# A two-layer conv/pool trunk on one core: low parts by subtraction, a later spill of x, and another place for the statistics of B's layer norm

## The chip, the cores and the metric

One NeuronCore of a Trainium2 chip runs the whole program. The metric is the device time of one execution in microseconds; the kernel before took 1789.1, 1791.0 and 1783.0 us in three runs (median 1789.1). Engines are named as the profile names them: PE is TensorE, DVE is VectorE, ACT is ScalarE, POOL is GpSimd, SP is SyncE, which issues most of the loads.

## What is computed

`x` is 1024 tokens by 1024 channels, fp32. Layer 0 mixes tokens with a Conformer convolution, layer 1 with a multi-scale pool; each is followed by a dense SwiGLU feed-forward of inner size 2816. Every sub-layer is normalized, shifted and scaled by numbers that come from a conditioning vector `c`.

```python
def conformer_conv(h, w1, b1, w_dw, b_dw, ln_g, ln_b, w2, b2):
    u = h @ w1 + b1
    a, g = jnp.split(u, 2, axis=-1)
    u = a * jax.nn.sigmoid(g)
    u = lax.conv_general_dilated(u, w_dw[:, None, :], ..., feature_group_count=D_MODEL) + b_dw   # 31 taps
    u = jax.nn.silu(layer_norm(u, ln_g, ln_b))
    return u @ w2 + b2

def swiglu_ffn(h, w_gate, w_up, w_down):
    return (jax.nn.silu(h @ w_gate) * (h @ w_up)) @ w_down

def reference(x, c, ada_w, ada_b, ...):
    c_act = jax.nn.silu(c)
    for i in range(DEPTH):
        mod = c_act @ ada_w[i] + ada_b[i]
        sh_m, sc_m, g_m, sh_f, sc_f, g_f = jnp.split(mod, N_ADA, axis=-1)
        h = modulate(rms_norm(x, norm_mix_g[i]), sh_m, sc_m)
        y = conformer_conv(h, ...) if i % 2 == 0 else multiscale_pool(h, ...)
        x = x + (1.0 + g_m)[:, None, :] * y
        h = modulate(rms_norm(x, norm_ffn_g[i]), sh_f, sc_f)
        x = x + (1.0 + g_f)[:, None, :] * swiglu_ffn(h, ...)
    return rms_norm(x, final_g)
```

## The kernel before, in words

**Tiles and products.** Channels lie on partitions, tokens along the free axis, in two chunks A and B of 512 tokens. A value that goes into TensorE is split into a high part, rounded to the matmul type by ScalarE, and a low part, the rest. Every product (`products`, L458) is then three matmuls of 128x128 by 128x512: high by high, high by low, low by high. These three are a row in what follows.

**Weights.** `load_weight` (L443) brings a slice of 128x1024 in fp32 into one of three `raw` buffers, and ScalarE casts it into the high part of one of five weight slots. The low part comes in one of two ways. With `summed=True`, ScalarE writes the negated copy of raw as the low part's input and a second DMA, issued by GpSimd's queue, loads the same slice again and accumulates it (tile `w<-in_..._dram`). Otherwise a subtract does it (`w<-raw,w`), on VectorE or GpSimd, whichever is free first by the program's model (`either`, L161). `run_units` (L591) decides: a unit names its weights, and a plain source is loaded with `summed=True`, while a callable in its place is called. Down weights are callables, and all others but the joint ones are plain sources.

**Order.** The program is written as a list of units that stands in TensorE's order: heads, down products, mixers. Work beside them (taps of the convolution, norms, the dots of `c` with the conditioning weights) is a generator that gives up control with a word. `pace` (L198) steps these while VectorE's or GpSimd's modelled clock is less than 4 us ahead of TensorE's. A word of `LOAD` holds a task back for that many us of the modelled clock, a word of `DELAY` (`DELAY_BEHIND` late in the program) until that long after its last instruction. `STRETCH` multiplies the modelled price of the taps of chunk B in the feed-forward of layer 0. The other engines' order comes from a list scheduler.

**Stages around the change.** Layer 0: `heads` computes pairs of gate and up slices (tile `p`, weights `wgu`) for A and B in rounds of four pairs, and after each round the down products of A (`dn<-g,w`, weights `wdn`). In the meantime the taps of B run on VectorE (`ca`) and on GpSimd and ScalarE (`pa`, `pr`). Then `layer_norm_silu` (L786) normalizes B over channels: a matmul with ones gives the mean, VectorE subtracts it (`u<-u,mean`), squares are added (`acc`), a matmul gives the variance, twelve small VectorE operations its inverse root, and another matmul spreads it (`rstd<-ident,col`); VectorE scales, ScalarE applies silu, and the high and low parts (`v`) go into the products with w2 (`conv_out`, L841, tile `y<-v,w`). After that come `whole` and `combinations` (L1098), which make sums of A's and B's halves, and the joint feed-forward of both chunks (`joint`, L1033, tiles `a`, `e`), down products of A and B, the pool of A beside the down products of B (`pool_h`, `pool_mixed`, L885, and `pool_out`, L911: tiles `win`, `mx`, `y<-mx,w`, weights `wpl`), the heads of layer 1 with the pool of B beside them, and again combinations, joint and down products. `ending` (L1214) is the last down product, with its own order.

**Spill.** `x_out` (L304) stores a chunk's x in four DMAs (`xd<-x`) on SP's queue, and `x_in` brings it back later; the buffers serve the combinations in between.

**Dots.** For layer 1, VectorE multiplies 48 slices of the conditioning weights with `c` (`adaw<-adaw,cact`); each slice is loaded by SP. They run from the joint stage of layer 0 on.

Of the kernel before, what the change touches and what calls it, by code (L numbers as in the profile page):

```python
# [38 lines left out]
ROUND = 4  # L39
# [12 lines left out]
DIAGS = 8  # L52
LOAD = {"load": 4.0, "slow": 6.0, "next": 4.0, "dots": 4.0}

ON_DVE = (1, 4)
AHEAD = 4
STRETCH = 1.35
LATER = 300
DELAY = {"stats": 2.75, "spread": 3.0}
DELAY_BEHIND = {"stats": 8, "spread": 4}  # L60

# [59 lines left out]
def trunk(ctx, tc, xT, c, vec, ada, adan, w1f, w1, wdg, w2, wgu, wdn, wpl, out):  # L121
# [356 lines left out]

    def mean_rsqrt(acc, n, keep=False):

        count = n // P
        yield "stats"
        b = bank("var")
        for i in range(count):
            matmul(b[:, i : i + 1], acc[:, i * P : (i + 1) * P], ones[:, 0:1], start=True, stop=True)
        v, t = b[:, :count], b[:, 16 : 16 + count]
        V_.tensor_scalar(v, v, EPS, None, op0=ADD)  # L490
        col = tmp.tile([P, 16], F32, tag="col1", name=nm("col"), bufs=1)[:, :count]
        yield from rsqrt(v, col, t)
# [95 lines left out]
    def unit(emit, *weights):  # L588
        units.append((weights, emit))

    def run_units(cap, early):  # L591
# [194 lines left out]
    def layer_norm_silu(ch):  # L786

        n = ch.n
        vs = [st["u", ch.i, k][:, HALO:] for k in range(KT)]
        acc = None  # L790
# [10 lines left out]
        if ch.i:  # L801
            calm[0], stretch[0] = True, 1.0
            clock["V"] = clock["G"] = clock["PE"]
        yield "stats"
        b = bank("mean")
# [7 lines left out]
        acc = yield from sum_sq([vs[k] for k in CENTRED], n)  # L813
        rstd = yield from mean_rsqrt(acc, n)
        S_.activation(tmp.tile([P, 16], F32, tag="col0", name=nm("col"), bufs=1)[:, 0:1], acc[:, 0:1], AF.Silu)
# [25 lines left out]
    def conv_out(ch, squares, then=None):  # L841
# [17 lines left out]
        for ds in [(0, 1), *((d,) for d in range(2, KT))]:  # L859
            unit(emit_of(ds), *[w2[d] for d in ds])  # L860
            if then is not None and len(ds) > 1:
                unit(then)
# [48 lines left out]
    def pool_out(ch, l, pair, sq):  # L911
        def emit(take):
            wt = take()
            for gi in range(2):
# [8 lines left out]
                pace()  # L923
        unit(emit, wpl[pair])

# [19 lines left out]
    def gated(l, i, f, g, u, kept=False):  # L945

        t = temp(512)
        S_.activation(t, g, AF.Silu)
        V_.tensor_tensor(t, u, t, op=MUL)
        both = block("u0", "g")  # L950
        split(t, both)
        if kept:
            st["g", i, f] = both[:, 0], both[:, 1]
        else:
            sync.dma_start(gd[l][i][f], both.bitcast(F32))

    def head(l, fp, kept=False):
# [24 lines left out]

        return (first, wgu[l, fp, 0]), (second, wgu[l, fp, 1])

# [113 lines left out]
    def combinations(l, squares):  # L1098

        hb = st["hb"] = [block("h1", "hb", F32) for _ in range(4)]  # L1100
        T = st["T"] = {name: {} for name in ("t1", "t2", "n3", "b22", "n4")}
        rstd = yield from mean_rsqrt(squares.acc, 512)
        lk = l * KT
# [84 lines left out]
    def down(ch, l, fs, then=()):  # L1188
# [19 lines left out]
        wd = []  # L1208
        unit(half(0, wd), *[lambda f=f: load_weight(wdn[l, f]) for f in fs])
        for emit in then:  # L1210
# [3 lines left out]
    def ending(ch, l, fs):  # L1214
# [27 lines left out]
        def emit(take):  # L1242
# [26 lines left out]
            for _ in behind_it:  # L1269
                pass  # L1270
        return emit, tuple(wdn[l, f] for f in fs)

# [196 lines left out]
    def heads(l, n, first):  # L1469

        for r in range(2):
# [4 lines left out]
            down(A, l, [2 * q for q in fps])  # L1476
        unit(lambda take: x_out(A))
        if n > 2 * ROUND:
# [21 lines left out]
    def conv_b():  # L1500
        need("ln_b")
        sq_b = Squares(B, True)
        conv_out(B, sq_b, lambda take: T.__setitem__("whole", Task(whole(0))))
        unit(lambda take: st.__setitem__("sq", sq_b))
# [105 lines left out]
```

## Time and profile before

| | us | share |
|---|---|---|
| median of 3 runs | 1789.1 | |
| profiled execution, its own time | 1792.09 | |
| span of its trace | 1790.2 | |
| PE busy | 1715.2 | 96% |
| DVE busy | 1290.3 | 72% |
| ACT busy | 795.7 | 44% |
| POOL busy | 595.5 | 33% |
| DMA, mean of the span | 218 GB/s | |

The mean granted TensorE clock is 0.987. The tables of waits list, for an engine, how long it sat idle and which tile, made by whom at which line, ended the wait. In a timeline row stand the start and the length in us, the engine, the line, the operation with its tiles, their shapes, and how many instructions the row holds; in brackets stands the idle time ahead of it and what ended it. Nearly all rows have line L115 or L137, two helpers that record all operations, so the tile names tell the place.

### The profile page before, as it was taken

How to read it: one execution, taken by the hardware profiler on the slowest of the kernel's cores; microseconds unless marked ns; L12 is line 12 of the kernel's file. 1: busy time of each engine (PE TensorE's matmuls, PEld its weight loads, DVE VectorE, ACT ScalarE, POOL GpSimd, SP SyncE). 2: the span in 40 equal slices, each digit the busy share in tenths (PEclk: the TensorE clock that was granted, in tenths of full speed). 3: DMA queues.
4: the chain of work that ended last, by engine and by line, in shares of the span. 5: the costliest groups of instructions: out<-in, count | busy, mean ns of one | idle time of the engine just before them, and what ended most of it. 6: DMA issues, size and time to landing. Idle time of an engine off the chain costs nothing.

```text
span 1790.2 us, 21682 instructions
## 1 busy us (share of the span) xinstructions
PE 1715.2 (96%) x7714; PEld 1392.9 (78%) x7714; DVE 1290.3 (72%) x1807; ACT 795.7 (44%) x1081; POOL 595.5 (33%) x544
## 2 busy tenths in 40 slices
PE   7999989999898999999999999899999999999996
PEld 5777767778686788778888878687788888888885
DVE  8899888796549788788667966636966666554655
ACT  3678677765645332323222447435633333322223
POOL 4587767576110332423211703411022122100001
PEclk9999989999999999999999999999999999999998
DMA  7958969757894977878876558779677677566552
GB/s 292 292 156 242 225 168 254 199 139 215 248 269 127 293 252 249 267 213 276 332 261 235 173 143 234 190 221 266 187 221 202 173 209 198 197 217 220 179 201 69
DMA packets 112030, 389.64 MB, mean 218 GB/s; under 512 B 12209, under 2 KB 14385, under 8 KB 111922
## 3 DMA queue, kind: packets, MB, share of 16 engines
q1 hardware_dynamic: 91536, 316.94, 49.9%
q0 software_dynamic: 19296, 70.26, 22.0%
q8 instruction: 61, 1.00, 0.2%
q10 hardware_dynamic: 1090, 1.05, 0.2%
q14 instruction: 47, 0.39, 0.1%
HBM read 326.34 MB, written 61.87 MB: 217 GB/s over the span
## 4 chain that ended last, share of the span: by engine, by line
PE 66%; DVE 12%; DMA 11%; issue 5%; ACT 3%; POOL 3%; SPq 0%; DVEq 0%; ACTq 0%; POOLq 0%
PE dn L137 21%; PE a L137 16%; PE e L137 8%; PE p L137 7%; PE y L137 5%; DMA raw<-in_wgu_dram 4%; PE g L137 3%; DVE t L115 3%; PE first L137 2%; DVE w L115 2%; PE tap L137 2%; ACT w L115 2%; DMA adaw<-in_adan_dram 1%; DVE x L115 1%; DMA w<-in_wgu_dram 1%
## 5 line engine op out<-in xcount | busy, mean ns | idle before, releaser
L115 ACT CAST w<-raw 128x1024 fp32r<-128x1024 f32 x274 | 286.7, 1049 | 537.5 <-PE dn L137 212.0
L137 PE MATMUL dn<-g,w 128*128 128x512 f32 (+1 forms) x2160 | 484.6, 385 | 6.9 <-DMA w<-in_wdn_dram 3.1
L137 PEld LDWEIGHTS dn<-g,w 128*128 128x128 f32 x2160 | 398.4, 188 | 89.5 <-DMA w<-in_wdn_dram 3.3
L137 PE MATMUL p<-h,w 128*128 128x512 f32 x1056 | 249.4, 396 | 8.0 <-DMA w<-in_wgu_dram 5.3
L137 PE MATMUL a<-n,w 128*128 128x512 f32 x1056 | 250.0, 392 | 5.3 <-DVE r L115 2.6
L115 DVE TENSOR_TENSOR w<-raw,w 128x1024 fp32r<-128x1024 f32 x155 | 215.4, 1391 | 51.8 <-ACT w L115 50.6
L137 PEld LDWEIGHTS p<-h,w 128*128 128x128 f32 x1056 | 201.1, 191 | 52.2 <-DMA w<-in_wgu_dram 6.1
L137 PEld LDWEIGHTS a<-n,w 128*128 128x128 f32 x1056 | 198.8, 189 | 49.9 <-issue 2.6
L115 DVE SCALAR_TENSOR_TENSOR x<-dn,gains,x 128x512 f32<-128x512 f32 (+1 forms) x200 | 138.9, 725 | 117.6 <-PE dn L137 117.6
L115 POOL TENSOR_TENSOR pa<-pa,pr 128x512 f32<-128x512 f32 x150 | 212.4, 1507 | 12.6 <-ACT pr L115 10.5
L115 DVE SCALAR_TENSOR_TENSOR ca<-u,vecs,ca 128x512 f32<-128x512 f32 x255 | 176.8, 748 | 0.5
L1006 POOL DMA_DIRECT2D raw<-in_wgu_dram x44 | 38.9, 885 | 365.8 <-DVE t L115 136.5
L115 POOL TENSOR_TENSOR w<-raw,w 128x1024 fp32r<-128x1024 f32 x29 | 80.6, 2782 | 181.0 <-ACT w L115 181.0
L115 POOL TENSOR_TENSOR g<-t,g 128x512 fp32r<-128x512 f32 x66 | 106.9, 1637 | 90.1 <-ACT g L115 78.2
L137 PE MATMUL e<-b,w 128*128 128x512 f32 x528 | 124.1, 390 | 3.6 <-DVE t L115 3.6
L137 PE MATMUL a<-t,w 128*128 128x512 f32 x528 | 124.4, 390 | 2.5 <-ACT t L115 1.6
L137 PE MATMUL e<-t,w 128*128 128x512 f32 x528 | 123.2, 389 | 0.0
L137 PEld LDWEIGHTS e<-b,w 128*128 128x128 f32 x528 | 98.8, 188 | 25.5 <-DVE t L115 2.6
L137 PEld LDWEIGHTS a<-t,w 128*128 128x128 f32 x528 | 99.0, 188 | 24.4 <-ACT t L115 2.5
L137 PEld LDWEIGHTS e<-t,w 128*128 128x128 f32 x528 | 99.1, 188 | 20.6
L115 ACT ACTIVATE pr<-u,vecs 128x512 f32<-128x512 f32 x150 | 101.5, 717 | 24.8 <-POOL pa L115 16.4
L137 PE MATMUL y<-v,w 128*128 128x512 f32 x384 | 92.9, 401 | 10.9 <-ACT v L115 8.2
(160 smaller groups left out, 2069.2 us busy)
## 6 DMA issues: line engine op xcount, KB each, us to landing
raw<-in_wgu_dram SPq DMA_DIRECT2D x132, 512.0 KB, 5.3
raw<-in_wdn_dram SPq DMA_DIRECT2D x88, 512.0 KB, 6.0
gd<-g SPq DMA_DIRECT2D x72, 512.0 KB, 6.2
g<-gd SPq DMA_DIRECT2D x72, 512.0 KB, 5.1
adaw<-in_ada_dram SPq DMA_DIRECT2D x48, 512.0 KB, 5.8
w<-in_wgu_dram POOLq DMA_DIRECT2D x44, 512.0 KB, 9.6
raw<-in_wgu_dram POOLq DMA_DIRECT2D x44, 512.0 KB, 7.4
raw<-in_w_dram SPq DMA_DIRECT2D x36, 512.0 KB, 7.0
```

The costliest lines, as they stand in the source:

```text
L115: self.last = self.order(getattr(self.eng, name)(out, *args, **kw))
L137: last_mm[0] = nc.tensor.matmul(out, lhsT, rhs, start=start, stop=stop, skip_group_check=more).ins.name
L1006: order(nc.gpsimd.dma_start(w[i], wgu[l, fp, src], accum_op=ADD))
```

## The change

It has six parts.

1. `LOAD["slow"]` goes from 6 to 8: the dots of layer 1 are spaced wider until the down products of layer 0's A are through.
2. `STRETCH` goes from 1.35 to 1.2: taps of B are priced lower, so that more of them are put beside the same matmuls.
3. Two new words for the place of statistics: `"soon"` (0.5) for mean and variance of B's layer norm, `"later"` (5 or 8) for the combinations' variance.
4. `direct` gives a callable in place of a plain source, so that the low part comes by a subtract: for the w2 slices 2 to 7 of B, the two pool weights of each chunk, the first slice of every fourth pair of heads, and the last two down weights. In `down` it only replaces an equal lambda. By the order, 18 accumulating DMAs and 18 negated copies go, 2 of the new subtracts stand on VectorE, and 16 on GpSimd.
5. The low part of a kept head's `g` is always VectorE's work: 6 of these move from GpSimd.
6. In layer 0, x of A is stored between the w2 products of B instead of before the last heads.

```diff
-LOAD = {"load": 4.0, "slow": 6.0, "next": 4.0, "dots": 4.0}
+LOAD = {"load": 4.0, "slow": 8.0, "next": 4.0, "dots": 4.0}
...
-STRETCH = 1.35
+STRETCH = 1.2
...
-DELAY = {"stats": 2.75, "spread": 3.0}
-DELAY_BEHIND = {"stats": 8, "spread": 4}
+DELAY = {"stats": 2.75, "spread": 3.0, "soon": 0.5, "later": 5.0}
+DELAY_BEHIND = {"stats": 8, "spread": 4, "soon": 0.5, "later": 8}
...
-    def mean_rsqrt(acc, n, keep=False):
+    def mean_rsqrt(acc, n, keep=False, when="stats"):
...
-        yield "stats"
+        yield when
...
+    def direct(src):
+        return lambda: load_weight(src)
...
@@ layer_norm_silu
-        yield "stats"
+        yield "soon" if ch.i else "stats"
...
-        rstd = yield from mean_rsqrt(acc, n)
+        rstd = yield from mean_rsqrt(acc, n, when="soon" if ch.i else "stats")
...
@@ conv_out
-            unit(emit_of(ds), *[w2[d] for d in ds])
+            unit(emit_of(ds), *[direct(w2[d]) if ch.i and d > 1 else w2[d] for d in ds])
...
@@ pool_out
-        unit(emit, wpl[pair])
+        unit(emit, direct(wpl[pair]))
...
@@ gated
-        split(t, both)
+        split(t, both, V_ if kept else None)
...
@@ head
-        return (first, wgu[l, fp, 0]), (second, wgu[l, fp, 1])
+        way = direct if fp % ROUND == 0 else lambda src: src
+        return (first, way(wgu[l, fp, 0])), (second, wgu[l, fp, 1])
...
@@ combinations
-        rstd = yield from mean_rsqrt(squares.acc, 512)
+        rstd = yield from mean_rsqrt(squares.acc, 512, when="later")
...
@@ ending
-        return emit, tuple(wdn[l, f] for f in fs)
+        return emit, tuple(direct(wdn[l, f]) for f in fs)
...
@@ heads
-        unit(lambda take: x_out(A))
+        if l:
+            unit(lambda take: x_out(A))
...
@@ conv_b
-        conv_out(B, sq_b, lambda take: T.__setitem__("whole", Task(whole(0))))
+        def spilled(take):
+            x_out(A)
+            T["whole"] = Task(whole(0))
+        conv_out(B, sq_b, spilled)
```

On TensorE, the layer norm of B stood like this before; the `dn` rows are the second round's down products of A, the `p` rows the last heads before w2.

```order
L137 MATMUL dn_3939<-g_3927,w_3894 128x512 x3
L137 MATMUL mean_3998<-acc_3968,ones 128x512
L137 MATMUL dn_4007<-g_3697,w_3748 128x512 x3
...
L137 MATMUL dn_4057<-g_3927,w_3894 128x512 x3
L137 MATMUL p_4115<-h_2803,w_3932 128x512 x3
...
L137 MATMUL var_4144<-ones,acc_4016 128x1 x4
L137 MATMUL p_4115<-h_2807,w_4066 128x512 x3
...
L137 MATMUL rstd_4193<-ident,col_4150 128x128 x4
L137 MATMUL y_4261<-v_4200,w_4081 128x512 x3
```

And like this in the changed kernel:

```order
L137 MATMUL p_3822<-h_2808,w_3719 128x512 x3
L137 MATMUL mean_3926<-acc_3889,ones 128x512
L137 MATMUL dn_3946<-g_3714,w_3766 128x512 x3
...
L137 MATMUL var_4040<-ones,acc_3975 128x1 x4
L137 MATMUL dn_4026<-g_3894,w_3856 128x512 x3
...
L137 MATMUL rstd_4098<-ident,col_4046 128x128 x4
L137 MATMUL dn_4072<-g_3894,w_3856 128x512 x3
...
L137 MATMUL p_4162<-h_2801,w_3943 128x512 x3
...
L137 MATMUL y_4249<-v_4105,w_4094 128x512 x3
```

Before, 16 rows of down products stood ahead of the mean, 16 down and 8 head rows between mean and variance, 8 head rows between variance and rstd, and none between rstd and y. Now none of these down rows stands ahead of the mean, 20 stand behind it, 8 between variance and rstd, and 4 down and 16 head rows between rstd and y.

On VectorE, the rows ahead of the mean's subtraction were these; `acc` sums the channels, `t<-p` belongs to the last head before the down products:

```order
L115 TENSOR_TENSOR t_3924<-p_3801,t_3924 128x512
L115 TENSOR_TENSOR acc_3083<-acc_3083,u_2256 128x512
L115 TENSOR_TENSOR acc_3083<-acc_3083,u_1211 128x512
L115 TENSOR_TENSOR acc_3968<-acc_3083,u_1211 128x512
L115 SCALAR_TENSOR_TENSOR x_79<-dn_3936,gains,x_79 128x512
...
L115 TENSOR_TENSOR u_1428<-u_1428,mean_3998 128x512 x2
```

In the changed kernel:

```order
L115 TENSOR_TENSOR acc_3102<-acc_3102,u_1211 128x512
L115 TENSOR_TENSOR acc_3889<-acc_3102,u_1211 128x512
L115 TENSOR_TENSOR t_3891<-p_3724,t_3891 128x512
L115 TENSOR_TENSOR g_3894<-t_3891,g_3894 128x512
L115 TENSOR_TENSOR t_3935<-p_3822,t_3935 128x512
L115 TENSOR_TENSOR u_1428<-u_1428,mean_3926 128x512 x2
```

The sum now ends ahead of the last two heads' `t<-p`, the low part of a kept `g` stands on VectorE, and the subtraction of the mean comes ahead of the first evictions of the down products.

In pool(A), on VectorE of the changed kernel, the dots stand between the windows; before, none of them stood behind the first window:

```order
L115 SCALAR_TENSOR_TENSOR win_8028<-win_8028,hp_7690 128x511
...
L115 SCALAR_TENSOR_TENSOR adaw_7922,mod<-adaw_7922,cact 128x1024
L115 TENSOR_TENSOR w_8043<-raw_8041,w_8043 128x1024
L115 TENSOR_TENSOR mx_8033<-win_8028,mx_8033 128x512
L115 SCALAR_TENSOR_TENSOR win_8079<-win_8079,hp_7690 128x511
L115 SCALAR_TENSOR_TENSOR adaw_7985,mod<-adaw_7985,cact 128x1024
L115 TENSOR_TENSOR win_8088<-win_8087 128x512
L115 TENSOR_TENSOR mx_8084<-win_8079,mx_8084 128x512
```

Seven of the 48 dots stand there now, and on GpSimd five weight subtracts instead of two between the windows of A. The statistics of the combinations stand in TensorE's order where they stood, in both layers.

More of the change, by code (lines that the diff above doesn't have):

```diff
@@ L1208, in down @@
         wd = []
-        unit(half(0, wd), *[lambda f=f: load_weight(wdn[l, f]) for f in fs])
+        unit(half(0, wd), *[direct(wdn[l, f]) for f in fs])
         for emit in then:
```

## The prediction

> **What bounds it now.** I read the busy line first, then the table of what TensorE waited for, then the timeline at each long wait, then the chain of waits behind it.
>
> ```profile
> span 1790.2 us, 21682 instructions
> PE 1715.2 (96%) x7714; PEld 1392.9 (78%) x7714; DVE 1290.3 (72%) x1807; ACT 795.7 (44%) x1081; POOL 595.5 (33%) x544
> ```
>
> TensorE is busy for 1715.2 of 1790.2 us, and the change takes no matmul away. So at most the other 75 us are to be had, and only what ends a TensorE wait counts. Work on VectorE (72%) or GpSimd (33%) is free until it becomes the last arrival. The columns of the next view are total us, times, longest us.
>
> ```profile
> PE var L137 <- DVE acc L115: 12.7, 4, 6.2
> PE p L137 <- DMA w<-in_wgu_dram: 5.3, 2, 3.7
> PE e L137 <- DVE t L115: 3.6, 3, 1.8
> PE y L137 <- DMA w<-in_wpl_dram: 3.0, 2, 1.8
> PE dn L137 <- POOL g L115: 2.5, 2, 1.6
> ```
>
> The edits aim at four of these five rows, and at two waits of one time each that the timelines below name. The first row's 6.2 us belong to the layer-0 combinations, whose variance and rstd rows stand in the same place in TensorE's order before and after, "later" or not: I cost that edit at nothing, since nothing moves there to gain or lose.
>
> **Layer norm of B, the largest term.** The TensorE timeline there:
>
> ```profile
> 434.89 11.05 PE L137 MATMUL dn<-g,w 128*128 128x512 f32 x48
> 445.77 1.02 PE L137 MATMUL mean<-acc,ones 128*128 128x512 f32 x2
> 446.24 11.46 PE L137 MATMUL dn<-g,w 128*128 128x512 f32 x48
> 462.98 0.95 PE L137 MATMUL var<-ones,acc 128*128 128x1 f32 x8
> 469.31 1.05 PE L137 MATMUL rstd<-ident,col 128*128 128x128 f32 x8
> 478.61 5.56 PE L137 MATMUL y<-v,w 128*128 128x512 f32 x16 [8.25 <-ACT v L115]
> ```
>
> Nothing stands between rstd and y, so the whole normalization (VectorE scales, ScalarE applies silu and rounds) lies open: 8.25 us. What ended it is on ScalarE and in the chain:
>
> ```profile
> 460.53 14.02 DMA raw<-in_w_dram
> 474.64 1.04 ACT L115 CAST w<-raw 128x1024 fp32r<-128x1024 f32 x1 [6.12 <-DMA raw<-in_w_dram]
> 476.55 1.50 ACT L115 ACTIVATE t<-u,vecs 128x512 f32<-128x512 f32 x2
> ```
>
> The first silu stood behind the cast of a w2 slice whose load took 14.02 us; without it the silu was due right after VectorE began to scale at 470.40. Now the clock on both sides of the wait (third column from the right in each row):
>
> ```profile
> 478.60:482.00 3.40, 3.39 (x8) 2.41 (x9) 2.16 (x4) 3.40 (x7) 0.00 (x0) 0.54 1.03 359
> 482.00:485.40 3.40, 3.40 (x17) 2.78 (x16) 1.91 (x4) 3.40 (x7) 0.00 (x0) 1.00 1.04 296
> ```
>
> After the wait 8 matmuls fit where 17 fit at clock 1.00, so the wait also costs 9 x 0.2 = 1.8 us: 10.05 us together. In the changed order the mean comes 48 matmuls (11.05 us) earlier, 60 down matmuls stand between mean and variance, 24 between variance and rstd, and 12 down and 48 head matmuls, 13.8 us at this rate, between rstd and y. These cover the 8.25 us and the late cast. What is late next is the mean, then the variance; VectorE shows both:
>
> ```profile
> 407.96 0.69 DVE L115 TENSOR_TENSOR t<-p,t 128x512 f32<-128x512 f32 x1 [6.91 <-PE p L137]
> 436.82 3.46 DVE L115 TENSOR_TENSOR acc<-acc,u 128x512 f32<-128x512 f32 x3
> 446.84 4.87 DVE L115 TENSOR_TENSOR u<-u,mean 128x512 f32<-128x512 f32 x8
> 458.98 0.68 DVE L115 TENSOR_TENSOR acc<-acc,t 128x512 f32<-128x512 f32 x1
> 470.40 4.87 DVE L115 TENSOR_TENSOR u<-u,rstd 128x512 f32<-128x512 f32 x8 [4.06 <-PE rstd L137]
> ```
>
> The channel sum ended at 436.82 + 3.46 = 440.28, and the mean now wants it at 434.89: it must come 5.4 us sooner. VectorE sat idle for 6.91 us before 407.96 because its next taps were not yet due; STRETCH 1.2 puts them there. VectorE's new order has the whole sum ahead of the last head's t<-p, where it stood behind it before. I take the mean as on time. From mean to the last square the work took 458.98 + 0.68 - 445.77 = 13.9 us, against 60 matmuls or 13.8 us now, with evictions mixed in: 1.2 us of wait at the variance, and 0.8 us for the rest of this chain. Term: +8.0 us; bounds -1 (all waits return one row earlier) and +10.05.
>
> **Direct low parts.** Eighteen weight slices lose a negated copy on ScalarE and an accumulating load, and get a subtract.
>
> ```profile
> w<-in_wgu_dram POOLq DMA_DIRECT2D x44, 512.0 KB, 9.6
> L115 DVE TENSOR_TENSOR w<-raw,w 128x1024 fp32r<-128x1024 f32 x155 | 215.4, 1391 | 51.8 <-ACT w L115 50.6
> L115 POOL TENSOR_TENSOR w<-raw,w 128x1024 fp32r<-128x1024 f32 x29 | 80.6, 2782 | 181.0 <-ACT w L115 181.0
> ```
>
> The low part is ready after 1.39 us on VectorE or 2.78 us on GpSimd instead of about 9.6 us. The words of the change say VectorE, but by the order 16 of the 18 land on GpSimd and 2 on VectorE: 16 x 2.782 = 44.5 us more on GpSimd. At the end of the kernel this pays in full:
>
> ```profile
> 1757.62 5.62 DMA w<-in_wdn_dram
> 1763.29 0.98 PE L137 MATMUL dn<-g,w 128*128 128x256 f32 x6 [3.10 <-DMA w<-in_wdn_dram]
> ```
>
> A subtract started where the 5.62 us load was issued ends 2.84 us sooner on GpSimd and 4.2 on VectorE; there the 3.10 us go whole. I take +3.1 (bounds +2.8 and +3.1). In the heads the direct slices are the first of every fourth pair, and the two weight waits in the p row (3.7 and 1.6 us) are at pair 5, which is not among them: 0. In layer 0 a first-round low part of g now queues on VectorE, and the spill's fourth piece of x is issued on SP behind four raw loads instead of two. In the whole trace one instruction waited for a piece of the spill, and that was in layer 1:
>
> ```profile
>   DVE af L115: 3.7, 1
> ```
>
> In layer 0 the stretch from the w2 products to the combinations hides it; without that cover it costs a wait of this kind. I take -1.0 for both (bounds -4 and 0).
>
> **Layer-1 heads around pool(B).** The two waits for g in the table above lie here, 2.5 us together, and one for a weight.
>
> ```profile
> 1120.63 4.97 DVE L115 SCALAR_TENSOR_TENSOR win<-win,hp 128x512 f32<-128x512 f32 x1 [2.75 <-POOL win L115]
> 1121.24 2.81 POOL L115 TENSOR_TENSOR g<-t,g 128x512 fp32r<-128x512 f32 x2
> 1127.86 1.16 DVE L115 SCALAR_TENSOR_TENSOR win<-win,hp 128x512 f32<-128x512 f32 x1
> 1154.60 5.76 PE L137 MATMUL p<-h,w 128*128 128x512 f32 x18 [3.73 <-DMA w<-in_wgu_dram]
> ```
>
> Six low parts of g go to VectorE, which is the faster one where no GpSimd work overlaps. I take +1.5, a bit over half of the 2.5 us, as VectorE is itself queued behind the pool's windows; bounds -1 and +6.2 (the 3.73 us too, should the loads before it run lighter).
>
> The first row bears on the whole change: this VectorE operation took 4.97 us while GpSimd worked on two tensors, and 1.16 us soon after. The Trainium skill's page "SBUF — State Buffer", section "Who interferes with whom", says that a VectorE instruction with two SBUF inputs and a GpSimd instruction that reads SBUF exclude each other for the length of an instruction; the 4.97 us agree, the mean of 1391 ns for 155 subtracts (many of them 1.22 us) says that such meetings are rare. By the rule at its worst, 16 subtracts that each hold VectorE on the path for 2.78 us, the sum would come out at 1777.0 + 44.5 = 1821.5, an estimate; by the mean it stays as it stands here.
>
> **The dots of layer 1.** LOAD slow 8 spaces these out, so they end later.
>
> ```profile
> L115 DVE SCALAR_TENSOR_TENSOR adaw<-adaw,cact 128x1024 f32<-128x1024 f32 x64 | 90.6, 1417 | 0.6 <-DMA adaw<-in_ada_dram 0.6
> 736.32 1.23 DVE L115 TENSOR_TENSOR raw<-raw,s 128x1024 f32<-128x1024 f32 x1 [3.88 <-DMA raw<-in_wgu_dram]
> 985.00:1048.00 63.00, 62.78 (x277) 51.41 (x275) 54.95 (x66) 23.89 (x31) 37.07 (x41) 1.00 0.56 171
> L115 DVE TENSOR_TENSOR mx<-win,mx x8: 676/684/1590, 996.8 to 1030.8; 128x512 fp32r<-128x512 f32 x8
> 1042.19 6.05 PE L137 MATMUL y<-mx,w 128*128 128x512 f32 x26
> ```
>
> In the joint products of layer 0 VectorE stops in order at a raw weight that is late (3.88 us in the second row), and e waits (3.6 us in all). A quarter fewer dot loads lie in its way: I take +2.5 (bounds 0 and +3.6).
>
> The price comes in pool(A), 985 to 1048. By the order seven dots now lie between its windows, 7 x 1.417 = 9.9 us, and five GpSimd subtracts instead of two, 3 x 2.782 = 8.3 us; VectorE is free for 63.0 - 54.95 = 8.05 us in that stage, and the rstd that starts it comes 12 matmuls (2.8 us) later. The last mx ended at 1031.5 and the first is used at 1042.19, so there are 10.7 us of slack, more for the later tiles. If windows alternate between the two engines the delays add, 9.9 + 8.3 + 2.8 = 21 us; if each hides in the other's idle time, 10. I take the low half, and give the wpl weight wait of 1.2 us back against it: -2.0 (bounds -12 and +1.2). In pool(B) the 1.8 us for wpl go, but the variance behind it waits for a chain that starts with a load of the spill:
>
> ```profile
> 1218.24 14.12 DMA xd<-x
> 1236.58 1.87 PE L137 MATMUL var<-ones,acc 128*128 128x1 f32 x8 [2.52 <-DVE acc L115]
> ```
>
> Its last piece stands behind one more raw load than before, so what wpl gives is asked back here: 0 (bounds -4 and +3).
>
> **Sum.** 8.0 + 3.1 - 1.0 + 1.5 + 2.5 - 2.0 + 0 = 12.1 us. The profiled execution took 1792.1 us (the span and 1.9 us around it), so it would become 1780.0; the median of the three runs is 3.0 us lower, so I forecast **1777.0 us**.
>
> **Rivals.** *Given back in place*: the channel sum or the squares are not ready, and the mean or the variance takes over the wait of y. For it: 5.4 us are to be made up and the variance has no reserve. Against: 6.91 us of idle VectorE. Then the first term is near 0: 1777.0 + 8.0 = 1785.
>
> *Slower, by pool(A) and pool(B)*: the windows alternate between VectorE and GpSimd, so dots and subtracts add up. Deciding point: the last mx more than 10.7 us later. At 21 us TensorE waits 10.3 us, and 1.8 more for the clock; in pool(B) three new subtracts do the same without slack, 8.3 + 1.8. That is 22.2 in place of my 2.0, so 1797; with the norm given back too, 1805. For it: the 4.97 us row. Against: the mean of 1391 ns, and 26 us of idle GpSimd in that stage. The skill's lock rule, named above, is the form in which I would expect it.
>
> *All of it pays*: 10.05 + 3.1 + 6.2 + 3.6 + 3.0 = 26.0 us less, 1763.1. For it: each of these waits is named in a row; against: another arrival is close behind most of them.
>
> **Chances.** The forecast, 1770 to 1784, gets 0.48; given back 0.22; slower 0.16; all of it 0.14. About 0.5%, 8.9 us, is what a measurement of this kernel can tell from no change, so the bounds are 1780.2 and 1798.0. Faster: three quarters of the forecast, all of the last, and a little of the second, 0.52. Slower: two thirds of its case and a little of the second, 0.13. Same: 0.35. The range leaves out half of the slow case and a part of the best: 1763 to 1797.
>
> **What would show it.** Right: no y<-v wait and clock 1.00 after it; no dn wait for wdn near the end; fewer e waits for t in layer 0; the last mx within 10 us of its old distance to y. Wrong: a mean or variance wait over 3 us at the layer norm (rival one); y waiting for mx, or VectorE windows near 5 us beside GpSimd subtracts (rival two). A new wait at the layer-0 combinations would overturn my zero for them.

## The result, and the profile after

The changed kernel takes 1804.1 us (median of five runs, 1798.0 to 1805.3) against 1789.1 us before: the ratio is 1.0083, 95% interval 1.0058 to 1.0108. It is slower by 15 us where the prediction had it 12 us faster, and outside the range of 1763 to 1797 us. The profiled execution took 1805.3 us. Its page, and what TensorE waited for (total us, times, longest us):

```profile
span 1803.5 us, 21651 instructions
PE 1726.4 (96%) x7714; PEld 1399.9 (78%) x7714; DVE 1315.9 (73%) x1815; ACT 778.3 (43%) x1062; POOL 610.8 (34%) x536
```

```profile
PE var L137 <- DVE acc L115: 18.1, 6, 5.4
...
PE e L137 <- DVE t L115: 9.3, 5, 4.0
PE p L137 <- DMA w<-in_wgu_dram: 4.2, 2, 2.1
PE a L137 <- DVE r L115: 3.8, 3, 2.0
PE dn L137 <- DVE g L115: 3.3, 2, 2.2
...
PE dn L137 <- POOL w L115: 2.3, 1, 2.3
PE dn L137 <- DVE x L115: 1.9, 1, 1.9
```

The wait of y for v is gone, and so are the waits for wdn and wpl. The wait of e for t has grown from 3.6 to 9.3 us, and down products now wait for g and x from VectorE and for a weight's subtract on GpSimd. The 18.1 us of the first row are six places; those that grew by much are pool(A)'s variance (from 0 to 2.67) and pool(B)'s (from 2.52 to 5.44). Both programs have the same 7714 matmuls in the same order but for the statistics of the layer norm and one rstd just ahead of pool(A), so the time of the n-th matmul says where the time went. In this table, worked out from the traces, stands what a stage took before, and by how much more or less it took in a run (us; "joint" are layer 0's joint products, from 5 us behind their start on, "pools' heads" are the first heads of layer 1):

```
stage, its start before     before   after  slow6  no direct  soon  slow8  calm  next2  slow4
start            2.6         405.0    -0.7   -1.5     -1.3    5.5   -2.9  -3.6    2.2    3.1
layer norm B   407.7         110.8    -7.6   -7.5     -2.0    1.9   -1.2  -7.4   -8.0   -7.5
joint, layer 0 552.5         306.1    12.6    2.8      8.8    4.6   13.9  -5.3   17.0   21.1
down A and B   858.6         130.0     0.7    0.0      0.8    0.0    0.4   1.1    6.3   -0.3
pool(A)        988.6          96.2    10.1   -1.5      7.6   -0.5    6.5   5.9    3.0   -1.7
pools' heads  1084.8         109.8     0.0    1.2     -4.2    0.3   -2.6   1.3    1.7    0.3
pool(B)       1194.6         123.8     1.0    1.4     -4.0   -4.2   -4.3   0.8   -0.6    1.4
end           1736.0          47.1    -3.4   -3.4      1.3    1.0    2.6  -3.4   -3.4   -3.4
```

Stages left out differ by nothing. The start runs the same matmuls in every kernel and still moves by -3.6 to +5.5 us, so that much is chance there; later stages repeat better (the end at -3.4 in five runs). The joint stage stands at +4.6 and +1.6 in two kernels that change nothing in it (`e3`, and `e13` below), so differences of that size there say nothing. Pool(B) has two values: of four kernels that change nothing in it three stand at -4.2 or -4.3 (`e3`, `e4`, `e13`) and one at 0.0 (`e16`), so the kernel before had bad luck of some 4 us there in its profile. Two stages hold the loss: the joint stage, 12.6 us, and pool(A), 10.1 us.

**The layer norm** went as planned. TensorE's timeline after:

```profile
434.62 1.02 PE L137 MATMUL mean<-acc,ones 128*128 128x512 f32 x2
449.92 1.05 PE L137 MATMUL var<-ones,acc 128*128 128x1 f32 x8 [0.66 <-DVE acc L115]
456.37 1.05 PE L137 MATMUL rstd<-ident,col 128*128 128x128 f32 x8
466.34 5.73 PE L137 MATMUL p<-h,w 128*128 128x512 f32 x24 [0.73 <-ACT r L115]
471.91 1.29 PE L137 MATMUL y<-v,w 128*128 128x512 f32 x5
```

The mean does not wait, the variance waits 0.66 us, and y not at all. The last down products run through as well; before, a wait of 3.10 us cut them:

```profile
1754.82 29.64 PE L137 MATMUL dn<-g,w 128*128 128x512 f32 x164
```

**The joint stage** lost its time like this. The rows are of VectorE, GpSimd (three), SP (two), VectorE and TensorE, in this order:

```profile
657.85 6.68 DVE L115 TENSOR_TENSOR w<-raw,w 128x1024 fp32r<-128x1024 f32 x1
...
658.27 2.70 POOL L115 TENSOR_TENSOR w<-raw,w 128x1024 fp32r<-128x1024 f32 x1
660.63 2.81 POOL L115 TENSOR_TENSOR g<-t,g 128x512 fp32r<-128x512 f32 x2
666.87 3.12 POOL L115 TENSOR_TENSOR w<-raw,w 128x1024 fp32r<-128x1024 f32 x1 [3.43 <-ACT w L115]
...
652.71 8.61 SPq L942 DMA_DIRECT2D raw<-in_wgu_dram  x2
...
670.02 0.33 SPq L942 DMA_DIRECT2D raw<-in_wgu_dram  x1
...
675.22 1.23 DVE L115 TENSOR_TENSOR raw<-raw,s 128x1024 f32<-128x1024 f32 x1 [6.30 <-DMA raw<-in_wgu_dram]
...
679.47 3.89 PE L137 MATMUL e<-b,w 128*128 128x512 f32 x9 [4.00 <-DVE t L115]
```

A subtract on VectorE took 6.68 us, while a subtract and two low parts of g ran on GpSimd, to 663.4. The second of SP's two raw loads waited 7.9 us, until the first of these GpSimd subtracts had ended at 660.97. Its slice is the one that GpSimd's next subtract reads (666.87 to 669.99), and only behind that did SP issue, at 670.02, the load of the slice that VectorE then missed: it landed at 675.09. So VectorE waited 6.30 us for a raw slice, and TensorE 4.00 us for VectorE. The path of the late slice goes through GpSimd's two subtracts: the long one on VectorE ended at 664.5, before the slice between them had landed (665.5).

The whole stage in one row, before and then after (us; busy time of PE, PEld, DVE, ACT and POOL; clock, DMA share, GB/s):

```profile
552.50:858.60 306.10, 297.94 (x1302) 243.29 (x1301) 258.53 (x296) 102.58 (x137) 102.81 (x69) 1.00 0.78 248
```

```profile
544.60:863.30 318.70, 303.67 (x1301) 246.49 (x1300) 244.82 (x273) 101.48 (x137) 113.81 (x72) 0.98 0.71 224
```

Of the 12.6 us, TensorE's idle time is 6.9 (from 8.2 to 15.0); the other 5.7 are the same matmuls at a mean clock of 0.98 instead of 1.00. Behind the wait of 4.00 us, for one, the clock stood at 0.50 for 3.3 us.

The groups of weight subtracts between 600 and 860 us, before and then after (busy us, mean ns; then idle time ahead of them):

```profile
L115 DVE TENSOR_TENSOR w<-raw,w 128x1024 fp32r<-128x1024 f32 x29 | 55.1, 1901 | 5.9 <-ACT w L115 5.9
...
L115 POOL TENSOR_TENSOR w<-raw,w 128x1024 fp32r<-128x1024 f32 x11 | 29.5, 2683 | 42.5 <-ACT w L115 42.5
```

```profile
L115 DVE TENSOR_TENSOR w<-raw,w 128x1024 fp32r<-128x1024 f32 x23 | 46.2, 2010 | 0.8 <-ACT w L115 0.8
L115 POOL TENSOR_TENSOR w<-raw,w 128x1024 fp32r<-128x1024 f32 x15 | 38.2, 2545 | 60.6 <-ACT w L115 60.6
```

Four more subtracts on GpSimd and six fewer on VectorE in this window; in the whole stage of the table it is 17 instead of 11 on GpSimd, and 27 instead of 33 on VectorE. None of them is an edit's own: `direct` touches no joint weight. The program chooses the engine by its modelled clocks, and the dots move these clocks. Of SP's waits between 600 and 860 us, those for a subtract on GpSimd grew from 33.5 to 44.9 us, and VectorE's waits for raw from 15.8 to 28.3 us:

```profile
SPq L939 <- POOL w L115: 33.5, 8, 7.4
...
DVE raw L115 <- DMA raw<-in_wgu_dram: 15.8, 5, 4.3
```

```profile
SPq L942 <- POOL w L115: 44.9, 12, 8.2
...
DVE raw L115 <- DMA raw<-in_wgu_dram: 28.3, 5, 6.8
```

**Pool(A)**, on VectorE, GpSimd and TensorE of the changed kernel:

```profile
1028.63 2.83 DVE L115 TENSOR_TENSOR mx<-win,mx 128x512 fp32r<-128x512 f32 x1
...
1032.70 3.08 DVE L115 SCALAR_TENSOR_TENSOR adaw<-adaw,cact 128x1024 f32<-128x1024 f32 x1
...
1027.60 3.31 POOL L115 TENSOR_TENSOR w<-raw,w 128x1024 fp32r<-128x1024 f32 x1
...
1032.32 2.38 POOL L115 TENSOR_TENSOR w<-raw,w 128x1024 fp32r<-128x1024 f32 x1
...
1030.97 20.53 PE L137 MATMUL dn<-g,w 128*128 128x512 f32 x82 [2.35 <-POOL w L115]
...
1066.34 3.71 PE L137 MATMUL dn<-g,w 128*128 128x512 f32 x15 [1.92 <-DVE x L115]
...
1072.72 1.87 PE L137 MATMUL var<-ones,acc 128*128 128x1 f32 x8 [2.67 <-DVE acc L115]
```

A window product that takes 0.68 us alone took 2.83, a dot 3.08 instead of 1.22, each beside a subtract on GpSimd. VectorE fell behind: counted from the start of the stage, the last mx ended 16.8 us later than before (at 1053.7). But y did not wait for mx: the waits came at a down weight, at the evictions of y, and at the sum of squares for the variance behind it. The stage in one row, before and then after (PE, PEld, DVE, ACT, POOL busy, clock, DMA share, GB/s):

```profile
988.60:1084.80 96.20, 94.24 (x421) 77.29 (x420) 78.91 (x114) 47.07 (x65) 42.27 (x54) 1.00 0.57 157
```

```profile
994.00:1100.40 106.40, 99.11 (x422) 80.71 (x421) 96.33 (x129) 45.80 (x63) 56.14 (x58) 0.95 0.51 161
```

VectorE had 17 us to spare and now has 10 in a longer stage; GpSimd does 14 us more. TensorE's idle time grew from 2.0 to 7.3 us; the other 4.9 us of the loss are the same matmuls at clock 0.95 instead of 1.00. Behind the waits of 2.35 and 2.67 us the clock stood at 0.51 and 0.50 for 3.3 us, behind the one of 1.92 us at 1.00.

### The profile page after: what moved, and what is told of

Same layout as the page of the kernel before. It is cut to its first block, busy times and chain, and to the rows that moved or that the text cites. A ratio compares the mean times of both kernels' runs of the same rounds, so it can differ in the third digit from the quotient of the medians.

```text
span 1803.5 us, 21651 instructions
## 1 busy us (share of the span) xinstructions
PE 1726.4 (96%) x7714; PEld 1399.9 (78%) x7714; DVE 1315.9 (73%) x1815; ACT 778.3 (43%) x1062; POOL 610.8 (34%) x536
## 4 chain that ended last, share of the span: by engine, by line
PE 64%; DVE 17%; DMA 9%; POOL 4%; issue 4%; ACT 2%; SPq 0%; DVEq 0%; ACTq 0%; POOLq 0%
PE dn L137 19%; PE a L137 15%; PE p L137 9%; PE e L137 7%; PE y L137 5%; DMA raw<-in_wgu_dram 5%; DVE t L115 3%; PE g L137 3%; DVE w L115 3%; PE first L137 2%; POOL pa L115 2%; PE tap L137 2%; DVE adaw L115 2%; DVE win L115 2%; DVE acc L115 2%
## 5 line engine op out<-in xcount | busy, mean ns | idle before, releaser
L137 PE MATMUL dn<-g,w 128*128 128x512 f32 (+1 forms) x2160 | 489.9, 388 | 7.5 <-DVE g L115 3.3
L115 POOL TENSOR_TENSOR pa<-pa,pr 128x512 f32<-128x512 f32 x149 | 212.9, 1518 | 12.6 <-ACT pr L115 10.3
L115 POOL TENSOR_TENSOR w<-raw,w 128x1024 fp32r<-128x1024 f32 x45 | 118.7, 2639 | 241.9 <-ACT w L115 241.8
L115 POOL TENSOR_TENSOR g<-t,g 128x512 fp32r<-128x512 f32 x60 | 96.1, 1630 | 75.0 <-ACT g L115 67.1
```

Of the source, the lines that this page charges most:

```text
L115: self.last = self.order(getattr(self.eng, name)(out, *args, **kw))
L137: last_mm[0] = nc.tensor.matmul(out, lhsT, rhs, start=start, stop=stop, skip_group_check=more).ins.name
```

## The experiments

Each run is compared with runs of the kernel before on the same chip; "joint" and "pool(A)" are stages of the table.

**Slow at 6** (`e1`): the changed kernel with one number back.

```diff
-LOAD = {"load": 4.0, "slow": 8.0, "next": 4.0, "dots": 4.0}
+LOAD = {"load": 4.0, "slow": 6.0, "next": 4.0, "dots": 4.0}
```

> The changed kernel with LOAD slow back at 6, all other parts kept. Theory D (the dots): the wider spacing of the layer-1 dots causes both losses that the aligned traces show, about 13 us in the joint stage of layer 0 and about 11 us from pool(A) to its variance; without it both go, and the time is near 1804 - 24 = 1780 us. Theory S (the subtracts): the losses come from the 16 more weight subtracts on GpSimd, which delay g, its spill and the raw loads queued behind it; then this kernel stays near 1801 us.

Measured: 1776.8 us, ratio 0.9927 (0.9903 to 0.9952). Joint +2.8 instead of +12.6, pool(A) -1.5 instead of +10.1. Theory D holds: this number alone turns a gain into a loss.

**No direct** (`e2`): w2, pool weights, heads and ending by accumulating loads.

```diff
-*[direct(w2[d]) if ch.i and d > 1 else w2[d] for d in ds]
+*[w2[d] for d in ds]
-unit(emit, direct(wpl[pair]))
+unit(emit, wpl[pair])
-way = direct if fp % ROUND == 0 else lambda src: src
+way = lambda src: src
-return emit, tuple(direct(wdn[l, f]) for f in fs)
+return emit, tuple(wdn[l, f] for f in fs)
```

> The changed kernel with every new use of direct taken back (w2, wpl, heads, ending by accumulating loads again); dots at 8, the layer norm's new place and the moved spill stay. Theory D: both losses stay, and the 3.4 us of the last down weights come back as a wait, so near 1807 us. Theory S: both losses go, and the time is near 1804 - 24 + 3.4 = 1783 us.

Measured: 1803.7 us, ratio 1.0076 (1.0046 to 1.0106). Joint +8.8, pool(A) +7.6: theory S falls, the new direct slices are not the main cause. Not foreseen: the layer norm gained 2.0 us only.

**Soon alone** (`e3`): the kernel before with `DELAY["soon"]` and the two `yield`s of B's layer norm.

> The kernel before with the word soon for B's layer norm alone. Both theories: the wait of y for v goes and TensorE runs some 7 to 8 us earlier from there to the end, 1789 - 7.5 = 1781.5 us. A rival: without the denser taps the channel sum comes too late, the mean waits up to 5.4 us, and little is gained (1787 us).

Measured: 1796.8 us, ratio 1.0026 (1.0005 to 1.0048). The norm took 1.9 us more, not 7.5 less. The rival had the right sign and the wrong place: the mean was on time, y waited as before for v, behind a late load of a raw w2 slice:

```profile
485.15 1.52 PE L137 MATMUL y<-v,w 128*128 128x512 f32 x2 [6.26 <-ACT v L115]
...
466.88 14.19 DMA raw<-in_w_dram
```

**Slow at 8 alone** (`e4`): the kernel before with `"slow": 8.0`.

> The kernel before with LOAD slow at 8 alone. Theory D: the losses of the joint stage and of pool(A) appear by themselves, 1789 + 15 to 24 = 1804 to 1813 us. Theory S: no such loss, 1786 to 1791 us, as the dots only come later.

Measured: 1813.2 us, ratio 1.0116 (1.0081 to 1.0150). Joint +13.9, pool(A) +6.5. Theory D: the number alone makes both losses. Its profiled execution was the fastest of four (1804.1 us), so the stages add up to less than the median's loss. Against the 10.1 of the full change, the direct slices add some 2.5 (from `e2`) to 3.6 us in pool(A).

**Calm** (`e5`): dots at 8, but the joint weights of layer 0 with all subtracts on VectorE.

```diff
-unit(lambda take: calm.__setitem__(0, False))
+unit(lambda take: calm.__setitem__(0, l == 0))
...
 unit(lambda take: lax.__setitem__(0, True))
+unit(lambda take: calm.__setitem__(0, False))
```

> The changed kernel with all weight subtracts, and the sums ahead of them, of layer 0's joint stage and of the down products of A behind it on VectorE (none chosen by the program's model); dots at 8. Theory G: the wider dots cost in the joint stage because more subtracts land on GpSimd there (15 to 16 instead of 9 to 11, at 2.5 us each), raw buffers come free late, and the raw loads behind them on SP arrive late; then the joint loss of about 13 us goes, and since VectorE's program order pushes all 7 or more dots still into pool(A), that loss stays or grows: 1790 to 1796 us. Theory V: the loss comes from the dots' places between VectorE's joint work or from their loads on SP; then it stays, and more work on VectorE makes it worse, 1805 to 1820 us.

Measured: 1785.9 us, ratio 0.9966 (0.9945 to 0.9987). Joint -5.3, pool(A) +5.9 with nine dots in it. The joint loss is gone with the dots still at 8, as theory G has it, and V falls; the time lies below G's range, since pool(A) lost less than in the change, not more. The edit takes more from GpSimd than the weights' subtracts: the 28 low parts of g in the joint stage, and the sums of raw slices, go to VectorE too, and GpSimd is busy for 17.4 us there instead of 113.8. That it is the subtracts which matter rests on the kernels beside it, in which the low parts of g on GpSimd are 28 or 29 whatever the loss. The subtracts of that stage, 600 to 860 us:

```profile
L115 DVE TENSOR_TENSOR w<-raw,w 128x1024 fp32r<-128x1024 f32 x38 | 46.5, 1223 | 23.2 <-ACT w L115 23.0
```

VectorE does 38 subtracts in 46.5 us; with 15 on GpSimd it needed 46.2 us for 23. Handing subtracts to GpSimd has freed nothing here.

**Next at 2** (`e6`): `"next": 2.0` in the changed kernel, so that all but two dots precede pool(A)'s windows.

> The changed kernel with LOAD next at 2 instead of 4, so that behind the down products of A the dots follow each other twice as fast and all but two stand ahead of pool(A)'s windows; the joint stage as in the change. Theory P: the loss of about 11 us from pool(A) to its variance comes from the dots between the windows; it goes, and the joint loss stays: about 1793 us. Rival: it comes from the GpSimd weight subtracts there, whose count is not smaller here; then the time stays near 1803 us.

Measured: 1805.3 us, ratio 1.0096 (1.0069 to 1.0122). Pool(A) fell from +10.1 to +3.0, as theory P says, with all seven GpSimd subtracts of that stage in place; but the time did not follow. The down products ahead of it took 6.3 us more: TensorE waited 2.3 us for a variance behind the packed dots, and the next 42 matmuls took 12.1 us instead of some 9.8. Joint stood at +17.0. Moved, the dots cost elsewhere: the rival's time came, but not for its reason.

**Slow at 4** (`e10`): `"slow": 4.0` in the changed kernel.

> The changed kernel with LOAD slow at 4: the dots stand denser than before in the joint stage and all end ahead of pool(A). GpSimd gets 52 subtracts in the whole program (45 at 8, 37 at 6). Theory G: what counts in the joint stage is the number of subtracts on GpSimd, so a loss of 10 us or more is there again though the dots are early: 1785 to 1793 us. Theory V: dots that come earlier make VectorE's queue longer in the joint stage, loss by waits for t without late raw loads. Theory L: only lateness of the dots costs; then it is as good as at 6, 1777 us.

Measured: 1797.8 us, ratio 1.0061 (1.0033 to 1.0088). Joint +21.1, pool(A) -1.7. Early dots spare pool(A) and cost more in the joint stage, where 27 subtracts (600 to 860 us) are on GpSimd, and VectorE's own take 3.8 us each:

```profile
L115 POOL TENSOR_TENSOR w<-raw,w 128x1024 fp32r<-128x1024 f32 x27 | 73.8, 2738 | 54.2 <-ACT w L115 54.2
...
L115 DVE TENSOR_TENSOR w<-raw,w 128x1024 fp32r<-128x1024 f32 x10 | 37.6, 3762 | 0.0
```

The time is above G's and L's numbers, and L falls. The loss is not one of late raw slices: VectorE's waits for raw fell from 15.8 to 1.4 us (600 to 860 us), and TensorE waited for r, which VectorE makes:

```profile
PE a L137 <- DVE r L115: 18.4, 9, 3.8
...
DVE raw L115 <- DMA raw<-in_wgu_dram: 1.4, 1, 1.4
```

**Slow at 6, w2 by accumulating loads** (`e8`): the first pair of lines of the diff of `e2`, on `e1`.

> The changed kernel with LOAD slow at 6 and with B's w2 slices 2 to 7 by accumulating loads again. If the layer norm's gain of 6.6 us (aligned trace of the run with slow 6) needs the direct w2 slices, y waits again for a weight or a late load and half of it or more goes: 1780 to 1782 us. If the new places in the order alone make it: 1777 us.

Measured: 1788.6 us, ratio 0.9995 (0.9975 to 1.0015). The norm gained 0.9 us instead of 7.5, as y waited 4.0 us for accumulating loads of w2: it needs the direct slices. The time is longer than either number foreseen.

**Slow at 6 and calm** (`e9`): the edits of `e1` and `e5` together.

> The changed kernel with LOAD slow at 6 and, as in the run before, layer 0's joint subtracts all on VectorE. Theory G: both causes are gone. Against the kernel before: layer norm -7.5, joint stage about -5, pool(A) -1.5, end -3.4, the rest +2.5, so about 1774 us. Theory V (the joint gain of the run with dots at 8 came from there being fewer dots, 22 instead of 31): the joint stage is back at +3 and the time at 1781 us.

Measured: 1777.2 us, ratio 0.9916 (0.9886 to 0.9945). Norm -7.2, joint -4.3, pool(A) -0.8. Theory G: with no subtract on GpSimd the joint stage is the same at 6 (-4.3) and at 8 (-5.3). The time lies between G's and V's.

**w2 alone** (`e13`): the kernel before with `direct` for the w2 slices 2 to 7 of B.

> The kernel before with the w2 slices 2 to 7 of B direct, nothing else. The norm's order stays as it was, so rstd stands right ahead of y. If the late cast behind a 14 us load made the wait of y, and the direct slices remove it, most of the layer norm's gain comes already here: -5 to -7 us at the norm, 1783 us. If the new places in the order are needed as well, the chain from rstd to the first v stays open, some 6 us of wait remain, and the gain is below 3 us: 1787 us.

Measured: 1798.9 us, ratio 1.0028 (1.0011 to 1.0046); the norm took 5.9 us more, a loss that neither number foresaw. The chain from rstd to the first v stays open, and later ones with it:

```profile
467.37 1.16 PE L137 MATMUL rstd<-ident,col 128*128 128x128 f32 x8 [2.08 <-DVE col L115]
472.97 0.80 PE L137 MATMUL y<-v,w 128*128 128x512 f32 x1 [4.44 <-ACT v L115]
475.29 2.92 PE L137 MATMUL y<-v,w 128*128 128x512 f32 x6 [1.53 <-DVE v L115]
```

**Fewest direct slices** (`e14`): `e9` with the pool weights and all heads by accumulating loads (second and third pair of the diff of `e2`).

> As the run with slow 6 and the joint subtracts on VectorE, but with the pool weights and the heads' first slices by accumulating loads as before; only w2 and the last down weights stay direct. If the direct pool and head slices cost something around the pools (GpSimd subtracts between the windows), it is 1 to 5 us faster than that run: 1770 us. If they gain there, as the prediction had it for the heads (+1.5), it is 1 to 3 us slower: 1776 us.

Measured: 1778.9 us, ratio 0.9920 (0.9896 to 0.9945). Both effects at once: the pools' heads and pool(B) took 8.1 us less than before, against 1.4 less in `e9`; but the norm stood at +1.3, since the accumulating load of the first w2 slices came late. Its issue on GpSimd's queue stood behind that of another accumulating load, which waited for a raw slice (457.61 to 467.02):

```profile
480.02 10.15 PE L137 MATMUL y<-v,w 128*128 128x512 f32 x37 [6.11 <-DMA w<-in_w_dram]
```

**Slow at 4 and calm** (`e15`).

> The changed kernel with LOAD slow at 4 and layer 0's joint subtracts on VectorE. By itself slow 4 put 38 subtracts on GpSimd in the joint stage and cost 21 us there. Theory G: with none there the loss goes although the dots are densest: joint stage -5 to +3, in all 1772 to 1780 us. Theory V: dense dots cost by themselves, and the joint stage stays 10 us or more above the kernel before: 1788 us or more.

Measured: 1787.8 us, ratio 0.9960 (0.9939 to 0.9981). Joint +4.6, from +21.1: most of the loss at 4 goes with GpSimd's work (the 38 of the expectation are 30 weight subtracts and 8 sums of raw slices). But against -5.3 and -4.3 at 8 and 6 some 9 us are left that belong to the denser dots: a products wait 9.0 us for t. So the stage lies between theories G and V, and the time at V's.

**More on GpSimd** (`e16`): the kernel before, dots at 6, a bias in the choice.

```diff
-        return V_ if v <= g else G_
+        return V_ if v + bias[0] <= g else G_
```

> The kernel before, dots at 6 as they were, with one edit: in layer 0's joint stage the choice between VectorE and GpSimd adds 0.6 us to VectorE's side, so that about 13 more of the joint weights' low parts land on GpSimd (45 in the whole program instead of 29). Theory G: the number of subtracts on GpSimd is what the joint stage pays for, whatever the dots do; a loss of 12 to 20 us in that stage and 1804 to 1810 us in all. Theory S (the spacing itself costs, and the subtracts only go along with it): the joint stage stays within 5 us of the kernel before, 1790 to 1796 us.

Measured: 1798.9 us, ratio 1.0035 (1.0008 to 1.0062), joint +10.2. In the profile SP's waits for GpSimd's subtracts are 63.7 us. It is slower with the count alone changed, but by 6 us in the timed runs, less than theory G had it and more than theory S; the profiled execution (1807.1 us) was its slowest of ten. VectorE's waits for raw slices did not grow (22.5 us in the stage, 28.8 before). So the count is a cause, and not the whole measure: 24 subtracts in the stage here cost less than 17 in `e4`. Which ones they are must count too; that was not taken apart.

**The parts that paid** (`e17`): `e9` with the pool weights by accumulating loads, and direct head slices in layer 0 only.

```diff
-way = direct if fp % ROUND == 0 else lambda src: src
+way = direct if fp % ROUND == 0 and l == 0 else lambda src: src
```

> The parts that paid, together: the layer norm's new place, denser taps, the later spill, direct slices for w2, for the heads of layer 0 and for the last down weights, dots at 6, joint subtracts of layer 0 on VectorE; pool weights and the heads of layer 1 by accumulating loads. If the layer norm needs the direct first slice of the last heads as well as the w2 slices, its 7 us are there again beside the gains around the pools: against the kernel before -7.4 at the norm, -5 in the joint stage, -4 to -8 from pool(A) to the combinations, -3.4 at the end, 1769 us. If the norm's gain in the earlier runs had to do with the direct slices of layer 1, it stays near that of the run with the fewest direct slices, 1778 us.

Measured: 1770.7 us, ratio 0.9884 (0.9845 to 0.9924). Norm -7.0, joint -5.3, pools' heads -3.4, pool(B) -5.3, end -3.4. Its page and its joint stage:

```profile
span 1769.0 us, 21649 instructions
...
PE 1705.2 (96%) x7714; PEld 1384.8 (78%) x7714; DVE 1297.3 (73%) x1867; ACT 785.4 (44%) x1069; POOL 493.9 (28%) x484
```

```profile
565.00:850.00 285.00, 283.88 (x1253) 234.73 (x1252) 227.88 (x308) 92.73 (x121) 19.31 (x25) 1.00 0.80 261
```

TensorE is busy 283.88 of 285 us there, with GpSimd nearly unused. It beats the kernel before by 1.2% and the changed one by 33 us of the medians (of different chips).

## Why the prediction was wrong

**Layer norm of B: right in size, +8.0 predicted, +7.6 measured.** Variance 0.66 us instead of 1.2, the mean on time, no wait of y. What it missed is on what that rests. The order alone (`e3`) cost 1.9 us, direct w2 alone (`e13`) 5.9; order and taps without w2 (`e8`) gave 0.9, without the heads' slice (`e14`) lost 1.3. All together gave 7.0 to 8.0 in eight kernels. The step "These cover the 8.25 us and the late cast" counted the late load of w2 as covered; with accumulating loads ahead it is not.

**The end: right**, +3.1 predicted, 3.4 in every kernel with direct last slices, and none without.

**The combinations: right at zero, on a wrong reading.** Their stage ahead of the joint products did not move. But the wait of 6.2 us that the prediction places there is the variance of the first norm, at 12.55 us, in a part that the change does not touch; at the combinations TensorE waited for no variance before either.

**The joint stage: this step failed.** It read "A quarter fewer dot loads lie in its way: I take +2.5 (bounds 0 and +3.6)". Measured: -12.6. The loads' number was not what mattered. The runs show in its place that the spacing of the dots shifts the modelled clocks by which the joint weights' subtracts are dealt out (17 instead of 11 on GpSimd, from the number alone in `e4`), and that this costs: with the choice taken from GpSimd (`e5`, `e9`) the spacing at 8 is as good as at 6. The changed order showed this count in the joint stage. The prediction counted 16 new subtracts on GpSimd over the whole program as the direct slices' own and looked for their places in pool(A); six of the 16 are joint weights dealt anew.

How the subtracts cost is not the same in all kernels. In this table of the joint stage, worked out from the traces, "held" is what VectorE's instructions took beyond the shortest of their kind in any run, in sum, and "raw" is VectorE's waiting for raw slices (us):

```
                          before  after  no direct  slow8  next2  slow6  more on G.  slow4  calm  slow4, calm
subtracts on GpSimd           11     17         17     17     17     11          24     30     0            0
held                        49.7   53.0       51.2   49.1   44.9   49.0        69.9   78.9   4.6          6.2
raw                         28.8   36.5       41.8   42.7   42.9   24.4        22.5    7.6  25.3         22.0
stage, us more                     12.6        8.8   13.9   17.0    2.8        10.2   21.1  -5.3          4.6
```

In the four kernels with dots at 8 and the choice left to the model, VectorE is held about as long as before, and waits 8 to 14 us longer for raw slices. With still more subtracts on GpSimd (`e16`, `e10`) raw slices come no later, and VectorE is held 20 to 29 us longer. So the loss of the change goes with late raw slices, those of the other two with a VectorE that is held up. Not every wait in these sums delays TensorE, and why the slices are late at 8 and not in `e16` stays open.

**Their price was read from the wrong mean.** The prediction took 1391 ns, the mean of all 155 subtracts on VectorE, as a sign that meetings with GpSimd are rare. In the joint stage the mean was 1901 ns already before, and is 1223 in `e5`, where GpSimd has none. The rule on the Trainium skill's page "SBUF — State Buffer", section "Who interferes with whom", by which a VectorE instruction with two SBUF inputs and a GpSimd one that reads SBUF exclude each other, was set aside on that mean; 6.68 us for one subtract, and 3762 ns as the mean of ten in `e10`, agree with the rule. But by the table above this price was paid before the change as well, and the change raised its sum by 3.3 us only.

**Pool(A): the mechanism was named, the size was off**: -2.0 taken (bounds -12 and +1.2), -10.1 measured, near the rival's 10.3 + 1.8. Dots and GpSimd subtracts both count, as the rival had it: seven dots with four subtracts in the stage +6.5 (`e4`), two dots with seven subtracts +3.0 (`e6`), seven and seven +10.1, no dot and four subtracts -1.5 (`e1`). They do not simply add up: nine dots and seven subtracts lost only 5.9 (`e5`). The rival's deciding point came, with the last mx 16.8 us later against 10.7, and still y did not wait for mx: TensorE waited for a weight, evictions and the variance, and nearly half of the loss is the lower clock. That the number is near the rival's is in part luck.

**Layer-1 heads: +1.5 predicted, 0.0 measured.** The waits for g are now VectorE's (3.3 us instead of 2.5 on GpSimd). The runs without direct slices there (`e14`, `e17`) took 8 to 9 us less in the pools' heads and pool(B) together, of which some 4 are the bad luck of the kernel before in pool(B); the rest goes with these slices and the pool weights, which the prediction did not foresee.

**Pool(B): 0 predicted, -1.0 measured**, within the bounds. TensorE's wait for wpl went, and TensorE waits 5.44 us instead of 2.52 for the variance, whose chain starts with a piece of the spill (VectorE's wait for it: 4.9 us instead of 3.7). The -1.0 taken for layer 0's heads and spill can't be told from chance, and no instruction of layer 0 waited for a piece of the spill.

**The slower rival** gave 1797 us for pool(A) and pool(B), and 1805 with the norm's gain lost too. That the time came to 1804 is luck: the norm kept its gain, and half of the loss lay in a stage that no rival spoke of. Of the four signs of being right, two came (no wait of y for v, no wait for wdn at the end) and two did not (e's waits for t, and the place of the last mx).

## What to carry to other kernels

Where a program deals out work by a modelled clock, count for each stage what a changed number re-deals, on every engine, and not only what the edit names. Take the price of an operation from the stage in which it runs: a mean over the program hid that each subtract on VectorE cost 1.9 us there and 1.22 alone. Here work given to the slower of two engines that hold each other up freed nothing on the faster one. And count a wait of TensorE for more than its length where the granted clock falls behind it: in the joint stage 6.9 us of idle time came with 5.7 us of slower matmuls.

## What the runs showed of the hardware

One VectorE instruction lasted across several GpSimd instructions in a row: 6.68 us for a subtract that takes 1.22 alone, while GpSimd ran a subtract and two low parts of g to 663.4; VectorE ended 1.1 us after that. A dot beside a single subtract of GpSimd (1032.32 to 1034.7) ended 1.1 us behind it as well, although GpSimd's next window operation had begun. So in the first place VectorE went on only after a run of GpSimd instructions, in the second after one of them. In the joint stage VectorE's instructions took 49.7 us more than the shortest of their kind before the change, and 4.6 us more where GpSimd had next to nothing to do (`e5`).
